# Grouping small matmuls of two side jobs: sums along heads in runs of five, transposes of a head pair in one run, and a wider spacing of a third group

## The chip, the cores and the metric

One core of one Trainium2 chip. The core has TensorE (PE, with its weight loads PEld), VectorE (DVE), ScalarE (ACT), GpSimd (POOL), SyncE (SP), which issues most DMAs, and 16 DMA engines. The metric is device time of one execution in microseconds; the median of three runs before the change is 1024.82 us (1024.57 to 1025.02).

## The reference

Two groups of tokens, 512 latent tokens and 128 context tokens (640 together), go through one layer of a hybrid backbone: a modulated norm, four gated mixers side by side (a short convolution, a bidirectional recurrence called HGRN2, attention, a chunked gMLP), an output projection and a ConvFFN. Everything is fp32. Only two mixers matter here.

```
cum    = cumsum(log_f)                                # per head, chunks of the sequence
scores = einsum('bhctd,bhcsd,bhctsd->bhcts', q, k, exp(cum_t - cum_s))
o      = scores @ v + (q * exp(cum)) @ state          # forward and, flipped, backward
o      = (o_f + flip(o_b)) * rsqrt(mean(o*o)) ; y_b = o * norm_g * silu(g)
```

```
s = concat(q @ k_window + bias, q @ k_context)        # 16 blocks: 4 heads x 4 column groups
p = softmax(s) ; y_c = p_window @ v_window + p_context @ v_context
```

## The kernel before, in words

Products are made exact enough by splitting each fp32 operand into a high part and a remainder, both stored as fp32r, and multiplying three times (high x high, high x remainder, remainder x high). The layer is a list of *units* that run one after another: the input projections (units 0 to 25: two column tiles for each of ff, fb, q, i, g, dv, du, ck, cq, cv, ac, ax, ab), some gates (26 to 29), one long unit of gate pairs in an order written out by hand (from 30), then the output projection and the FFN. A projection unit is `gemm` (L362): two halves of 320 columns, eight steps of three products each. Units i and dv are `tok_tile` (L933), with products of 256 columns and 20 steps each.

Between those products run *side jobs*, Python generators: `hgrn` (the recurrence), `gmlp`, `conva`, `attn`, `ada_cols` (modulation columns, one by one, as dot products on DVE at L262) and `g_operands`. What sets the order is a planner's clock `now`. A gemm step adds 0.41 to it (`tick(0.41)`), a step of `tok_tile` 0.33, and a side job's own PE work adds what `pe(...)` says. After each tick every job that is due is advanced to its next `yield`. A yield of `x` makes the job due `x` times its slack after the clock at which that step began (slack 1.3 for `hgrn`, 1.1 for `attn`, 1.0 for `ada_cols`):

```
def step(j):
    j[0] = now[0] + (next(j[1]) or 0.0) * j[2]
```

What is issued in this order is then placed on each engine by the framework's scheduler: it keeps the order where an instruction's operands are ready by its own model of time and pulls later instructions ahead where they are not. On the chip each engine then runs its list in order. `tc.keep_in_program_order` fixes some instructions; L262's are among them. From unit 30 to the end of the gate pairs everything is fixed.

The places that matter:

- `along` (L460 to L470) multiplies each of ten 128x128 blocks of a tensor by `heads`, a matrix of two columns. It sums a product of query and key along the 64 rows of each head. It runs twice: on `ksum` (tile D, during units 6 and 7) and on `near` (tile E, during units 8 and 9). Each of its ten matmuls is two passes on PE (it is fp32, not fp32r), each with its own weight load.
- Then come seven levels of the recurrence (L526, two or more groups of small matmuls each, and products on DVE at L545 and L549), the states (L565, L574), the outputs of five token tiles (L619 to L631), their norm (DVE L635 and L304, POOL L305, DVE L610), and the last transposes (L648): for each of five token tiles two transposes into the two halves of one PSUM tile, each followed by a product on DVE (L652).
- `ada_cols` stops after a column while `hgrn_y` is set and `hgrn_done` is not, that is from the last normed tile to the end of those transposes.
- `attn` waits for the end of `hgrn` and works in eight iterations, each for a pair of heads: `s3` of the pair before (L864 to L871), `s1` of the next pair (POOL L819, PE L827 and L830, DVE L834 and L836, ACT L837), and `s2` for each head of this pair: reciprocal and scaling on DVE (L843, L844), three transposes (L847) and a copy (DVE L1931 for one head, ACT L1929 for the other).

## Time and profile before

| | us |
|---|---|
| median of three runs | 1024.82 |
| the profiled execution's own time | 1023.97 |
| its span, first to last instruction | 1022.1 |
| PE busy | 1008.3 |
| DVE busy | 790.1 |
| first and last sum along heads (L466), start | 76.9 and 101.9 |
| first and last of the last transposes (L648), start | 198.7 and 203.6 (weight loads) |
| first and last of attention's transposes (L847), start | 228.2 and 283.0 (weight loads) |

The lists of the profile read: start in us, duration, engine, line, operation, output <- inputs, shape, count; in brackets the idle time before it and what ended it. A busy PE is not a PE at its peak: matmuls are pipelined, so what one costs is read from the starts of its neighbours. Lines are those of the kernel; a matmul issued in `gemm` is L362, in `tok_tile` L933.

### The profile page before, as it was taken

The numbers are of one execution on the slowest core, as the hardware profiler recorded it, in microseconds if no ns is written. First come the engines' busy times: TensorE is split into PE (matmuls) and PEld (weight loads), VectorE is DVE, ScalarE is ACT, GpSimd is POOL, SyncE is SP. The second block draws the span as 40 slices with busy tenths as digits, with TensorE's granted clock in tenths as the row PEclk, the third lists the DMA queues.
The fourth block names the chain that finished last, engine by engine and source line by source line (L and its number), as shares of the span: only waits on it lengthen the run. The fifth ranks groups of instructions, "written<-read, shape, count | busy, mean of one in ns | idle before, by whom it ended". The sixth has DMA issues, their size and how long they took to land.

```text
span 1022.1 us, 18764 instructions
## 1 busy us (share of the span) xinstructions
PE 1008.3 (99%) x7572; PEld 951.9 (93%) x7572; DVE 790.1 (77%) x1308; ACT 538.6 (53%) x933; POOL 106.5 (10%) x153
## 2 busy tenths in 40 slices
PE   8999999999999999999999999999999999999997
PEld 6899999999899999999998899999999999888886
DVE  6758899769866676767868879998888887796644
ACT  6642343354555444444544567777777776634432
POOL 1000020312100000000010111111112221001101
PEclk9999999999999999999999999999999999999999
DMA  9864433597562413323179584765555669974212
GB/s 354 322 221 127 126 124 114 171 263 216 143 206 79 155 52 104 130 77 104 49 282 349 207 328 112 195 163 150 150 151 149 154 161 271 370 259 146 83 42 103
DMA packets 55926, 177.85 MB, mean 174 GB/s; under 512 B 8192, under 2 KB 14624, under 8 KB 53280
## 3 DMA queue, kind: packets, MB, share of 16 engines
q1 hardware_dynamic: 45008, 140.60, 39.6%
q0 software_dynamic: 10832, 36.06, 14.8%
q8 instruction: 59, 0.97, 0.4%
q14 instruction: 27, 0.22, 0.1%
HBM read 134.93 MB, written 25.46 MB: 157 GB/s over the span
## 4 chain that ended last, share of the span: by engine, by line
PE 91%; DVE 5%; DMA 1%; issue 1%; ACT 1%; POOL 1%; SPq 0%; POOLq 0%; DVEq 0%; ACTq 0%
PE g L1478 19%; PE m L1122 17%; PE g L362 14%; PE g L1813 8%; PE m L1813 6%; PE g L1135 5%; PE m L1478 4%; PE m L1262 3%; PE g L933 2%; PE g L1262 2%; PE m L148 2%; PE g L148 1%; PE m L1473 1%; PE m L526 1%; DMA A<-in_w_ada_dram 1%
## 5 line engine op out<-in xcount | busy, mean ns | idle before, releaser
L362 PE MATMUL g<-XH,w 128*128 128x320 f32 x704 | 171.4, 317 | 0.0
L362 PEld LDWEIGHTS g<-XH,w 128*128 128x128 f32 x704 | 120.6, 188 | 2.4 <-issue 1.2
L362 PE MATMUL g<-XL,w 128*128 128x320 f32 x352 | 108.8, 309 | 0.0
L362 PEld LDWEIGHTS g<-XL,w 128*128 128x128 f32 x352 | 66.3, 188 | 0.0
L311 DVE TENSOR_TENSOR w<-raw,w 128x1024 fp32r<-128x1024 f32 x34 | 41.4, 1221 | 14.9 <-ACT w L310 9.1
L1122 PE MATMUL m<-XH,w 128*128 128x320 f32 x224 | 52.5, 309 | 0.0
L1813 PE MATMUL g<-w,XH 128*128 128x512 f32 (+1 forms) x216 | 50.2, 385 | 0.0
L1813 PEld LDWEIGHTS g<-w,XH 128*128 128x128 f32 x216 | 39.5, 188 | 8.3 <-ACT XH L1772 0.3
L310 ACT ACTIVATE w<-raw 128x1024 fp32r<-128x1024 f32 x34 | 35.7, 1050 | 21.3 <-PE g L1262 10.0
L1813 PE MATMUL g<-w,XL 128*128 128x512 f32 (+1 forms) x180 | 42.4, 386 | 0.0
L148 DVE SCALAR_TENSOR_TENSOR X<-MG,p2t,X 128x641 f32<-128x641 f32 x44 | 38.9, 885 | 4.3 <-ACT X L148 3.4
L148 DVE SCALAR_TENSOR_TENSOR X<-X,p2t,X 128x641 f32<-128x641 f32 x44 | 38.9, 884 | 1.9 <-ACT X L148 1.0
L1813 PEld LDWEIGHTS g<-w,XL 128*128 128x128 f32 x180 | 33.4, 188 | 7.1 <-DVE dt L1828 0.2
L148 ACT ACTIVATE w<-raw 128x1024 fp32r<-128x1024 f32 (+3 forms) x46 | 38.2, 851 | 2.7 <-DMA raw<-in_w_in_dram 1.7
L1478 PE MATMUL g<-XL,w 128*128 128x320 f32 x240 | 38.6, 310 | 0.0
L1478 PE MATMUL g<-XL,C 128*128 128x320 f32 x240 | 38.4, 309 | 0.0
L1122 PEld LDWEIGHTS m<-XH,w 128*128 128x128 f32 x224 | 38.3, 188 | 0.0
L1478 PEld LDWEIGHTS g<-XL,w 128*128 128x128 f32 x240 | 36.0, 188 | 0.5 <-ACT MG L148 0.3
L1813 PE MATMUL m<-w,XH 128*128 128x512 f32 (+1 forms) x156 | 36.4, 381 | 0.0
L1478 PEld LDWEIGHTS g<-XL,C 128*128 128x128 f32 x240 | 35.9, 188 | 0.4 <-ACT MG L148 0.4
L1122 PE MATMUL m<-XL,w 128*128 128x320 f32 x112 | 34.6, 309 | 0.0
L1813 PEld LDWEIGHTS m<-w,XH 128*128 128x128 f32 x156 | 28.5, 188 | 5.6
(549 smaller groups left out, 2751.9 us busy)
## 6 DMA issues: line engine op xcount, KB each, us to landing
raw<-in_w_up_dram SPq DMA_DIRECT2D x30, 512.0 KB, 4.9
raw<-in_w_gp_dram SPq DMA_DIRECT2D x21, 640.0 KB, 4.0
raw<-in_w_down_dram SPq DMA_DIRECT2D x22, 512.0 KB, 4.0
raw<-in_w_in_dram SPq DMA_DIRECT2D x19, 512.0 KB, 4.2
H<-in_w_adt_dram SPq DMA_DIRECT2D x16, 512.0 KB, 4.5
actd<-X POOLq DMA_DIRECT2D x22, 320.5 KB, 5.4
X<-in_w_adt_dram SPq DMA_DIRECT2D x10, 512.0 KB, 4.0
upd<-XL SPq DMA_DIRECT2D x4, 1280.0 KB, 6.4
```

The costliest lines, as they stand in the source:

```text
L148: r = f(*args, **kw)
L310: act(w[0], raw, AF.Copy)
L311: vec.tensor_tensor(w[1], raw, w[0].bitcast(F32), ALU.subtract)
L362: mm(o, w[:, h, k0 + k, :], r(k)[:, s], start=(k == 0 and i == 0), stop=(k == kt - 1 and i == 2))
L526: mm(m[W * g:W * g + W, (i - s0) * W:(i - s0 + 1) * W], lhs, rhs, start=True, stop=True, tile_position=(64 * par, W * g))
L933: mm(o, x(kx)[:, ts], w[:, h, k, :], start=(kx == 0 and i == 0), stop=(kx == 7 and i == 2))
L1122: mm(o, w[:, k, :], x[:, k, :], start=(first and k == 0 and j == 0), stop=(k == 3 and j == 2), skip_group_check=True)
L1135: mm(pb[:, c, 0:HC], w[:, h + k, :], y[:, x, k, s], start=(k == 0 and j == 0), stop=(k == 1 and j == 2))
L1262: mm(m, mh[k // 2][:, hx, k % 2, t * P:(t + 1) * P], wo[q][:, hw, k % 2, :], start=(k == 0 and i == 0), stop=(k == 7 and i == 2))
L1473: mm(o, w[:, k, :], x[:, k, :], start=(first and not part and k == 0 and j == 0), stop=(part == 1 and k == 3), skip_group_check=True)
L1478: z = mm(o, w[:, k, :], x[:, k, :], start=(first and k == 0 and j == 0), stop=(k == 3 and j == 2), skip_group_check=True)
L1813: mm(ps, sl[k][hx][:, t * P:(t + 1) * P], w[:, hw, k, c0:c1], start=first, stop=end and (last or nh == 1 and t == 4 and kk_ == 7))
```

## The change

Three places, no arithmetic changed:

- `along` issues its ten matmuls in two runs of five, with a yield of 2.5 after each run, where each had its own yield of 0.5.
- The last transposes of the recurrence yield 0.8 after each token tile instead of 0.4.
- In attention both heads' `s2` are issued in one step, 0.6 after the point where the first was issued before; the yields of an iteration still add up to 5.3 (1.5 + 0.6 + 3.2 for 1.5 + 1.2 + 1.2 + 1.4).

```diff
@@ along
             for i in range(10):
                 mm(mv[:, i, :], x[:, i * P:(i + 1) * P], heads, start=True, stop=True)
                 pe(0.22)
-                yield 0.5
+                if i % 5 == 4:
+                    yield 2.5
             return m
@@ hgrn, after the two transposes of a token tile
                 vec.scalar_tensor_tensor(s, m[:, pr * P:(pr + 1) * P],
                                          p1[:, C_HN + pr:C_HN + pr + 1], s, ALU.mult, ALU.mult)
-            yield 0.4
+            yield 0.8
         nc.sync.dma_start(ybd, split_y("D", sg).bitcast(F32))
@@ attn
             yield HD[6]
-            for i in range(2):
-                s2(u + i)
-                yield 1.2
-            yield HD[8] - 0.6
+            yield 0.6
+            s2(u)
+            s2(u + 1)
+            yield HD[8] + 1.2
         s3(14)
```

`HD[6]` is 1.5 and `HD[8]` is 2.0.

## The prediction

> **What bounds the kernel now.** I read the page's head first, then the list of PE's waits, then the order of time around the three places.

> ```profile
> span 1022.1 us, 18764 instructions
> PE 1008.3 (99%) x7572; PEld 951.9 (93%) x7572; DVE 790.1 (77%) x1308; ACT 538.6 (53%) x933; POOL 106.5 (10%) x153
> PE 91%; DVE 5%; DMA 1%; issue 1%; ACT 1%; POOL 1%; SPq 0%; POOLq 0%; DVEq 0%; ACTq 0%
> ```

> PE is busy 99% of the span and holds 91% of the chain that ended last. So the change can act in two ways only: through the PE time that its matmuls take among the fp32r products, and through stalls of PE. The span of 1022.1 belongs to an execution of 1023.97 us, 0.85 below the median of 1024.82; I add up against 1023.97 and put the 0.85 on at the end.

> The stalls at the lines concerned, first from the view of L648 (the recurrence's last transposes), then from that of L847 (attention's):

> ```profile
> L648 PEld LDWEIGHTS m<-cst,MG x10: 137/138/142, 198.6 to 203.6; 128*128 128x128 f32 x10
>   DVE MG L652: 2.3, 2
> ```

> ```profile
> L847 PEld LDWEIGHTS m<-cst,X x48: 137/139/143, 228.2 to 283.0; 128*128 128x128 f32 x48
>   DVE X L844: 1.4, 4
>   DVE X L834: 0.3, 1
> ```

> These rows count one wait twice, on PE and on its weight loads; the list of waits by engine separates them:

> ```profile
> PE m L648 <- DVE MG L652: 1.0, 1, 1.0
> PE m L847 <- DVE X L844: 0.4, 2, 0.2
> ```

> That leaves 1.3 us at L648 (2.3 - 1.0) and 1.3 at L847 (1.4 + 0.3 - 0.4), 2.6 us in all. The view of the sums (L466) lists no idle time. So 2.6 us, 0.25% of the time, is all that better places for these matmuls can win.

> **The sums in runs of five: the price of an interruption.** PE in order of time, columns start, duration, operation:

> ```profile
> 77.53 0.28 PE L933 MATMUL m<-w,XH 128*128 128x256 f32 x1
> 77.65 0.28 PE L466 MATMUL m<-heads,D 128*128 128x2 f32 x2
> 77.79 0.36 PE L933 MATMUL m<-w,XH 128*128 128x256 f32 x1
> 78.00 0.28 PE L933 MATMUL m<-w,XL 128*128 128x256 f32 x1
> 78.12 0.28 PE L933 MATMUL m<-w,XH 128*128 128x256 f32 x1
> ...
> 80.00 0.28 PE L933 MATMUL g<-w,XH 128*128 128x256 f32 x1
> 80.11 0.50 PE L466 MATMUL m<-heads,D 128*128 128x2 f32 x4
> 80.48 0.36 PE L933 MATMUL g<-w,XH 128*128 128x256 f32 x1
> 80.68 0.28 PE L933 MATMUL g<-w,XL 128*128 128x256 f32 x1
> ```

> Undisturbed products start 0.12 apart (78.00, 78.12). With one sum between them, two gaps take 78.00 - 77.53 = 0.47, so the sum costs 0.47 - 0.24 = 0.23. Here chance has put two sums side by side: 80.68 - 80.00 = 0.68, so the two cost 0.44, 0.22 each. A run saves 0.01 per sum at most. The loss after a run (0.20 to 0.21 to the second product instead of 0.12) is there, but inside the run each pass waits for its own weights as long (80.48 - 80.11 = 0.37 for four passes, 0.14 for two). If that goes on for five, twenty sums gain 20 x 0.01 = 0.2 us; from below I take 0, from above the 16 run ends that go, at 0.09 each: 1.4 us. I take 0.1, since two is the nearest row to five.

> The transposes follow the same law, one and four in a run:

> ```profile
> 198.56 0.31 PE L362 MATMUL g<-XH,w 128*128 128x320 f32 x1
> 198.71 0.27 PE L648 MATMUL m<-cst,MG 128*128 128x128 f32 x1
> 198.74 0.40 PE L362 MATMUL g<-XH,w 128*128 128x320 f32 x1
> 198.97 0.31 PE L362 MATMUL g<-XL,w 128*128 128x320 f32 x1
> 199.12 0.31 PE L362 MATMUL g<-XH,w 128*128 128x320 f32 x1
> 199.27 0.27 PE L648 MATMUL m<-cst,MG 128*128 128x128 f32 x1
> 200.56 0.33 PE L648 MATMUL m<-cst,MG 128*128 128x128 f32 x1 [1.02 <-DVE MG L652]
> ...
> 208.95 0.31 PE L362 MATMUL g<-XH,w 128*128 128x320 f32 x1
> 209.09 0.60 PE L749 MATMUL m<-cst,G 128*128 128x128 f32 x4
> 209.45 0.39 PE L362 MATMUL g<-XH,w 128*128 128x320 f32 x1
> 209.68 0.30 PE L362 MATMUL g<-XL,w 128*128 128x320 f32 x1
> ```

> Undisturbed gap 0.15 (198.97 to 199.12). One: 198.97 - 198.56 - 0.30 = 0.11. Four: 209.68 - 208.95 - 0.30 = 0.43, again 0.11 each. Eight runs of six instead of sixteen of three: 0 us, bound 8 x 0.08 = 0.6.

> **The sums also move the whole recurrence.** By the planner's arithmetic a sum in `tok_tile` was due 0.65 after its start; its own 0.22 and two ticks of 0.33 pass that, so ten sums took 20 ticks. Now a run of five is due 3.25 after its start; its own 1.10 leaves 2.15, seven ticks, 14 for both runs. In gemm steps (0.41) it was two ticks again (0.22 + 0.41 falls short of 0.65), 20 in all; now 2.15 takes six, 12 in all. With six and eight ticks gained and some rounding, everything behind the sums comes 10 to 16 ticks earlier; the last transposes start 15 ticks earlier. A gemm tick is three products of 0.15, so 198.7 becomes about 192. Nothing waits for `hgrn` there: the work of units 10 to 19 is PE's own, and `attn` starts after unit 19 as before. Cost: 0, as long as DVE keeps up; what moves is which DVE work meets which.

> **The last transposes, 0.8 apart.** In clock, one tile took its 0.22 and one tick; now two ticks. Why PE stopped there is in DVE's list:

> ```profile
> 195.56 0.42 DVE L610 TENSOR_TENSOR MG<-MG,hss 128x256 f32<-128x256 f32 x1 [0.99 <-POOL hss L305]
> 195.90 1.49 DVE L663 TENSOR_TENSOR E<-X,E 128x1280 fp32r<-128x1280 f32 x1
> 197.31 1.22 DVE L262 SCALAR_TENSOR_TENSOR junk<-H,S 128x1024 bf16<-128x1024 f32 x1
> 198.57 1.22 DVE L262 SCALAR_TENSOR_TENSOR H<-H,S 128x1024 f32<-128x1024 f32 x1
> ...
> 200.16 0.61 DVE L652 SCALAR_TENSOR_TENSOR MG<-m,cst,MG 128x128 f32<-128x128 f32 x2
> 200.93 0.35 DVE L652 SCALAR_TENSOR_TENSOR MG<-m,cst,MG 128x128 f32<-128x128 f32 x1 [0.17 <-PE m L648]
> ```

> The third transpose waits for the first product L652, because it is the second half of the first tile's PSUM tile, which DVE is reading. That product started 1.45 after its transpose (198.71 to 200.16), behind L663 and two column products L262. The wider spacing does not touch this first wait: both halves of a tile are still issued in one step, and the column job's products are still free to fill DVE. It even takes away the other tiles' transposes that stood between two halves. Free of a queue, transpose to transpose takes 200.93 - 200.56 + 0.35 = 0.72; if the scheduler leaves three products between (0.44 plus 0.08 for the switch), each later pair waits 0.2. So from 1.3 us the stall goes to between 0 (DVE free at once) and 1.3 + 4 x 0.2 = 2.1, or more if more columns lie ahead (rival below); I take 1.7, +0.4, since the DVE queue of the same make stands there.

> **Attention's pairs.** In the clock, an iteration loses one tick (three roundings instead of four), so the last of eight comes about seven ticks, 3 us, earlier; PE's own work is the same. The first head's scaling gets 0.66 more clock before its transposes, the second 0.66 less. Where PE waited, DVE was full:

> ```profile
> 249.00:272.00 23.00, 22.48 (x165) 19.67 (x165) 21.23 (x56) 10.24 (x22) 6.15 (x8) 1.00 0.63 168
> ```

> (PE, PEld, DVE, ACT, POOL busy, then PE's clock.) DVE is busy 21.23 of 23.00 us. By the clock the column products, issued in the same steps as each `s2` before and ahead of it, now come one to four ticks after it in the first half of the iterations, which helps; denser iterations on a full DVE hurt. Bounds: all 1.3 gone, or as much again; I take -0.3. Copies and PSUM buffers are the same in number.

> Sum: -0.1 (sums) + 0 (move) + 0.4 (last transposes) - 0.3 (attention) = 0.0. So 1023.97 + 0.0 + 0.85 = 1024.8.

> [...]

> ```profile
> 178.00:189.00 11.00, 11.00 (x96) 11.00 (x94) 8.69 (x28) 2.63 (x8) 2.02 (x2) 1.00 0.53 155
> 1016.00:1022.10 6.10, 0.00 (x0) 0.00 (x0) 1.45 (x5) 0.72 (x1) 0.55 (x1) 0.68 0.36 146
> ```

> The clock does fall in this trace, to a mean of 0.68 after PE's last product; it stays 1.00 in the stretch from 178 to 189, the recurrence's outputs, with 96 matmuls of many small kinds. [...]

> **Rivals.** *A, the waits go* (0.13). The recurrence leaves the crowded place, the two scalings come ahead of the column products, and all 2.6 us go: 1022.2. For it: the waits hang on one DVE queue each. Against: 21.23 of 23.00 us busy.

> *B, DVE is late for the last transposes* (0.11). In the clock the column job now stops before a column that it finished before the transposes, so two columns instead of one stand ready to fill DVE just before them. If both are placed there, the first L652 is two products of 1.22 later: +2.4, and four later pairs at 0.2 bring 0.8: 3.2 more, 1028.0. It decides once the first L652 starts over 3 us after its transpose (1.45 now). Against: the scheduler fills only what it holds idle.

> *C, runs are cheap after all* (0.04): the 0.08 to 0.09 at each run's end goes, 16 x 0.09 + 8 x 0.08 = 2.0: 1022.8, or 0.2%. Against: the rows for two sums and four transposes.

> *D, PE's clock halves in the runs* (0.02): four runs of sums (1.1 each) and eight of transposes (0.67 each) take twice as long: 9.8, so 1034.6. Against: clock 1.00 in 178 to 189.

> **How the numbers follow.** The forecast, no change beyond 0.2% (about what a measurement of this kernel can tell from no change, 2.05 us), has 0.70: its terms are bounded by waits of 1 to 2 us each. Faster by over 0.2% is A, 0.13. Slower is B and D, 0.13. Within is the rest, 0.74, C at the edge included. The range of 1022.6 to 1027.4 takes in the bounds of the terms (2.6 down less a little, 0.8 + 1.3 up with some of B) and leaves out the far ends of A and B, and D.

> **What would show it.** Runs of ten passes at L466, 0.11 apart, with 0.22 for each sum: the price. L648 starting near 192 instead of 198.7: the move. A wait of PE for L652 of 1 to 2 us: the queue; none is A, over 3 is B. Six-fold rows at L847 with waits for L844 of together about 1 us. A stall of over 1 us at L526 or anywhere else between 70 and 290 that is not there now, or a start of the gate pairs moved by over 2 us, makes the prediction wrong.

## The result and the profile after

The changed kernel takes 1031.26 us (median of five executions, 1028.05 to 1032.82) against 1024.65 us before, measured beside it: the ratio is 1.0060 (95% interval 1.0048 to 1.0071). The prediction was 1024.8, with a range of 1022.6 to 1027.4. The profiled execution is the longest of the five; its span grew from 1022.1 to 1031.0 us, 8.9 us.

The head of its page, and from its list of PE's waits (total, times, longest) the two rows that matter here. The lines of the changed kernel below L468 have moved down by one: L527 is L526 of before, L649 is L648, L848 is L847.

```profile
span 1031.0 us, 18769 instructions
PE 1015.4 (98%) x7572; PEld 957.6 (93%) x7572; DVE 789.0 (77%) x1308; ACT 538.7 (52%) x933; POOL 110.8 (11%) x153
```

```profile
PE m L649 <- DVE MG L653: 2.3, 2, 1.4
PE m L527 <- DVE C L546: 1.6, 2, 1.1
```

There are the same 7572 matmuls, but PE's busy time grew by 7.1 us (1008.3 to 1015.4): the matmuls took longer. A wait at L527, the recurrence's levels, is new; that at L649 grew from 1.0 to 2.3 us; L848, attention's transposes, is no longer in the list.

Where the time went shows in busy time by stretch. The columns are the length, then PE, PEld, DVE, ACT and POOL with their instructions, PE's granted clock (1.00 is full speed), the DMA share and GB/s. The changed kernel first:

```profile
104.00:146.70 42.70, 42.60 (x1040) 39.98 (x1039) 37.20 (x67) 19.27 (x38) 7.22 (x6) 1.00 0.37 115
146.70:150.20 3.50, 1.95 (x27) 1.48 (x26) 3.50 (x6) 0.17 (x1) 0.00 (x0) 0.99 0.49 150
150.20:160.40 10.20, 10.20 (x86) 8.97 (x87) 5.92 (x12) 3.32 (x9) 0.00 (x0) 0.50 0.33 104
```

and the same stretches of the kernel before:

```profile
146.70:150.20 3.50, 3.50 (x27) 3.31 (x27) 3.50 (x6) 1.83 (x5) 0.00 (x0) 1.00 0.58 193
150.20:160.40 10.20, 10.20 (x148) 8.37 (x145) 9.24 (x21) 5.07 (x12) 0.00 (x0) 1.00 0.49 157
```

From 104 to 146.7 PE is as busy as before (42.60 us in both) and gets through as many matmuls (1041 before). Then PE stands for 1.6 of 3.5 us, and for the next 10.2 us its clock is granted at 0.50: 86 matmuls instead of 148, of several sizes. PE is busy all through these 10.24 us, so I put the price of half speed at half of them, 5.1 us. That is an estimate, and a little high for the products of `gemm`: three of them take 0.80 us there (156.40 to 157.20) where they take 0.44 at 1.00 (146.13 to 146.57), which by 0.36 of 0.80 gives 4.6.

The sum goes by two milestones, two of ACT's copies out of PSUM, here of the kernel before and then of the changed one:

```profile
103.67 0.71 ACT L409 ACTIVATE MG<-g 128x640 f32<-128x640 f32 x1 [0.68 <-PE g L362]
217.46 0.70 ACT L418 ACTIVATE MG<-g 128x640 f32<-128x640 f32 x1 [0.41 <-PE g L362]
```

```profile
104.19 0.71 ACT L409 ACTIVATE MG<-g 128x640 f32<-128x640 f32 x1 [0.90 <-PE g L362]
226.96 0.71 ACT L418 ACTIVATE MG<-g 128x640 f32<-128x640 f32 x1 [0.40 <-PE g L362]
```

By 104 us, when all sums along heads are done, it is 0.5 late; at the start of attention 9.5; at the end 8.9. So the 9.0 us are lost in between: 1.6 of waits at L527, 5.1 of clock, 2.3 - 1.0 = 1.3 of waits at L649. About 1 us is left (1.5 with 4.6 for the clock) that I cannot put on one place. After that 0.6 comes back: the last sigmoid of the gates stands at 317.85 against 309.49, 8.4 late, so the stretch with attention gives back 1.1, and 0.5 is lost again behind it.

The other four executions differ mostly in the clock. Their times and mean granted clocks are 1028.05 (0.998), 1029.05 (0.999), 1031.26 (0.995) and 1031.53 (0.995), and the profiled one 1032.82 (0.993). A mean clock that is lower by 0.003 is 3.1 us of 1031, one lower by 0.005 is 5.2. So by this estimate two executions kept their clock, two lost about 3 us to it and one 5; only the last has a trace. With the clock kept, the change costs 3.4 to 4.4 us; the rest is what the clock does.

**Why PE stopped at L527.** PE in order of time in the changed kernel, and below it DVE:

```profile
147.01 0.31 PE L362 MATMUL g<-XH,w 128*128 128x320 f32 x1
148.46 0.32 PE L527 MATMUL m<-C,B 64*64 64x64 f32 x2 [1.14 <-DVE C L546]
149.20 0.79 PE L527 MATMUL m<-C,B 64*64 64x64 f32 x18 [0.41 <-DVE C L546]
```

```profile
138.36 0.31 DVE L550 TENSOR_TENSOR A<-A 128x80 f32<-128x80 f32 x1
141.16 1.23 DVE L324 TENSOR_TENSOR w<-raw,w 128x1024 fp32r<-128x1024 f32 x1 [2.49 <-ACT w L323]
142.30 1.31 DVE L262 SCALAR_TENSOR_TENSOR junk<-H,S 128x1024 bf16<-128x1024 f32 x1
...
146.03 1.64 DVE L546 TENSOR_TENSOR B<-B,A 128x640 f32<-128x640 f32 x2
147.59 1.55 DVE L546 TENSOR_TENSOR C<-C,A 128x640 f32<-128x640 f32 x2
```

The last level (the 64x64 matmuls) needs four products of DVE, L546, which end at 149.14 (147.59 + 1.55). They stand behind three column products L262, and these behind L324, a weight's remainder, for which DVE sat idle 2.49 us: it needs ACT's copy L323. On ACT, changed kernel and then before:

```profile
137.05 2.99 ACT L542 ACTIVATE MG<-D 32x640 f32<-32x640 f32 x4 [1.68 <-DVE D L532]
140.06 1.06 ACT L323 ACTIVATE w<-raw 128x1024 fp32r<-128x1024 f32 x1
```

```profile
132.50 1.05 ACT L323 ACTIVATE w<-raw 128x1024 fp32r<-128x1024 f32 x1
139.14 2.99 ACT L541 ACTIVATE MG<-D 32x640 f32<-32x640 f32 x4 [3.31 <-DVE D L531]
```

The recurrence has moved forward past a weight's conversion: L323 used to stand ahead of the four copies of L542 and now stands behind them. So DVE delivers the block at about the same time as before (147.80 + 1.55 = 149.35 there), although the recurrence as a whole lies earlier. But PE has nothing left ahead of the level from 147.3 on, where it came to it at 152.4 before:

```profile
147.80 1.55 DVE L545 TENSOR_TENSOR C<-C,A 128x640 f32<-128x640 f32 x2
152.39 0.80 PE L526 MATMUL m<-C,B 64*64 64x64 f32 x20
```

**Why PE stopped longer at L649.** DVE around the last transposes of the changed kernel:

```profile
201.24 0.35 DVE L653 SCALAR_TENSOR_TENSOR MG<-m,cst,MG 128x128 f32<-128x128 f32 x1
203.30 1.23 DVE L262 SCALAR_TENSOR_TENSOR junk<-H,S 128x1024 bf16<-128x1024 f32 x1 [1.71 <-DMA H<-in_w_adt_dram]
204.45 0.60 DVE L653 SCALAR_TENSOR_TENSOR MG<-m,cst,MG 128x128 f32<-128x128 f32 x2
```

The first wait is that of before. The second is new: a column product got into DVE's queue between the first and the second product L653, and the weights that it reads had not landed. DVE stood 1.71 us for a DMA with the second and the third L653 behind it, and PE, at its fifth transpose (205.11), stood 1.43 us for the third.

### The profile page after: what moved, and what is told of

Read it like the earlier page. It is cut to its first block, busy times and chain, and to the rows that moved or that the text cites. A ratio compares the mean times of both kernels' runs of the same rounds, so it can differ in the third digit from the quotient of the medians.

```text
span 1031.0 us, 18769 instructions
## 1 busy us (share of the span) xinstructions
PE 1015.4 (98%) x7572; PEld 957.6 (93%) x7572; DVE 789.0 (77%) x1308; ACT 538.7 (52%) x933; POOL 110.8 (11%) x153
## 4 chain that ended last, share of the span: by engine, by line
PE 78%; issue 9%; DVE 5%; DMA 4%; ACT 2%; POOL 1%; SPq 1%; POOLq 0%; DVEq 0%; ACTq 0%
PE g L1479 19%; PE m L1123 17%; PE g L362 9%; PE g L1814 8%; PE m L1814 5%; PE g L1136 5%; PE m L1479 4%; PE m L1263 3%; PE g L1263 2%; PE m L1474 1%; DMA B<-in_w_ada_dram 1%; DMA S<-in_w_ada_dram 1%; DMA C<-in_w_ada_dram 1%; DVE D L586 1%; DVE junk L262 1%
## 5 line engine op out<-in xcount | busy, mean ns | idle before, releaser
L362 PE MATMUL g<-XH,w 128*128 128x320 f32 x704 | 171.8, 320 | 0.1
L362 PEld LDWEIGHTS g<-XH,w 128*128 128x128 f32 x704 | 122.1, 191 | 2.9 <-issue 1.0
L362 PE MATMUL g<-XL,w 128*128 128x320 f32 x352 | 110.4, 314 | 0.0
L362 PEld LDWEIGHTS g<-XL,w 128*128 128x128 f32 x352 | 67.3, 191 | 0.1
L323 ACT ACTIVATE w<-raw 128x1024 fp32r<-128x1024 f32 (+1 forms) x22 | 24.3, 1104 | 18.9 <-issue 8.8
```

The lines of the kernel that those rows point to most:

```text
L323: high = lambda: act(w[:, 0], raw, AF.Copy)
L362: mm(o, w[:, h, k0 + k, :], r(k)[:, s], start=(k == 0 and i == 0), stop=(k == kt - 1 and i == 2))
```

## The experiments

Each was timed in five rounds beside the kernel before, whose median was 1024.24 to 1024.39 us in all four series. Ratios are to the kernel before, with their 95% intervals.

**The sums in runs alone** (first part of the diff).

```diff
-                yield 0.5
+                if i % 5 == 4:
+                    yield 2.5
```

> The sums' part of the change alone: two runs of five with a yield of 2.5 after each, the transposes as before. Theory 'place': the loss is in where the recurrence comes to lie (14 to 16 planner steps earlier), so most of the 6.6 us stay: 1028 to 1032, with a stop of PE at L526 before its last level and executions in which PE's clock falls for about 10 us. Theory 'later parts': the loss is the spacing's and attention's, and this kernel stays within 1 us of 1024.7. Theory 'runs': as 'place' in time, told apart by e2 and e3.

1039.61 us, 1.0153 (1.0129 to 1.0177): this part alone costs 15.3 us, more than twice the whole change and well over the 1028 to 1032 that I expected. Its waits:

```profile
PE g L362 <- ACT gt L972: 3.4, 1, 3.4
PE m L865 <- DVE B L1932: 2.8, 1, 2.8
PE m L649 <- DVE MG L653: 2.5, 2, 1.6
PE m L527 <- DVE C L546: 1.3, 2, 0.8
```

The lower two are those of the changed kernel; the upper two are not in it. PE's clock falls behind two of the stops, for 6.83 and 3.41 us. ACT's order around the first wait:

```profile
292.07 0.28 ACT L871 ACTIVATE C<-m 128x128 fp32r<-128x128 f32 x1 [1.51 <-PE m L865]
296.35 0.42 ACT L148 ACTIVATE H<-raw 128x256 fp32r<-128x256 f32 x1 [4.00 <-DMA raw<-in_w_gp_dram]
296.78 1.28 ACT L972 ACT_TABLE_LOAD   x1
298.07 0.79 ACT L972 ACTIVATE gt<-g,cst 128x640 f32<-128x640 f32 x1
```

The gate's sigmoid, which must free a PSUM tile for PE, stands behind a copy whose DMA is late by 4.00 us.

**The same runs, in place**: longer yields, so that the recurrence stays where it was.

```diff
-        def along(x):
+        def along(x, wait):            # 3.3 for ksum, 3.9 for near
-                yield 0.5
+                if i % 5 == 4:
+                    yield wait
```

> Runs of five, but with yields of 3.3 and 3.9 after each, so that the planner reaches everything behind the sums at the same step as before (along ends at its 85th and 119th step in both). Theory 'place': 1024.4 to 1025.0, the price of a sum unchanged at 0.22 us and no new stop. Theory 'runs' (five sums in a row cost PE time or PE's clock): as slow as e1, 1028 to 1032.

1024.74 us, 1.0002 (0.9993 to 1.0011). There is no wait at the levels or the gate, attention's transposes wait 1.0 us (0.4 before), and the clock stays at 1.00 from its first rise to the last product. A run of five costs and saves nothing that this measurement can tell.

**Single sums, moved**: no runs, but yields short enough for the recurrence to come forward as in the first experiment.

```diff
-                yield 0.5
+                yield 0.5 if i % 5 in wait else 0.2      # wait: (1, 3) for ksum, (2,) for near
```

> Each sum alone among the fp32r products, but with shorter yields, so that the recurrence lies exactly where the runs put it (along ends at steps 79 and 106, as in e1). Theory 'place': 1028 to 1032 as e1, with the same stop before the last level. Theory 'runs': 1024 to 1025.5.

1034.75 us, 1.0095 (1.0079 to 1.0112), again over the 1028 to 1032 that I expected. DVE's idle time before L324 is there (2.46 us), and so is the stop at the gate:

```profile
PE g L362 <- ACT gt L971: 3.1, 1, 3.1
PE m L648 <- DVE MG L652: 1.8, 1, 1.8
```

With the run in place there is no loss, without runs but moved there is one: it is the move. Only the stop at L526 did not come. DVE's rows and the start of the level on PE show why not:

```profile
139.68 1.23 DVE L324 TENSOR_TENSOR w<-raw,w 128x1024 fp32r<-128x1024 f32 x1 [2.46 <-ACT w L323]
145.16 1.55 DVE L545 TENSOR_TENSOR C<-C,A 128x640 f32<-128x640 f32 x2
147.03 0.80 PE L526 MATMUL m<-C,B 64*64 64x64 f32 x20
```

L324 starts 1.5 us earlier than in the changed kernel, and two column products stand between it and the block instead of three. So the block is done at 146.71, and PE comes to the level at 147.03. DVE's idle time behind ACT is therefore not enough for the stop: it takes that and what DVE has queued in front of the block.

**Attention's pair alone** (third part).

> Attention's part alone: both heads' transposes in one step. From the trace of the changed kernel, whose delay shrinks by 0.6 us over attention and which lists no wait at attention's transposes any more: 0.3 to 1.3 us faster, 1023.4 to 1024.4. The forecast had put -0.3 on it; a rival with a fuller DVE: up to 1.3 us slower.

1024.97 us, 1.0004 (0.9995 to 1.0012): not the gain that I expected. The waits at L847 stay at 0.3 us in the list (0.4 before), and one of 1.1 us for the copy of DVE appears at the next place, `PE m L864 <- DVE B L1931`.

**The spacing alone** (second part).

> The kernel before with the last transposes 0.8 apart and nothing else changed. Theory (the loss comes from where the sums leave the recurrence, the spacing only moves four pairs by 0.2 us each): the waits at the last transposes stay within 0.5 us of before's 1.3 us, no fall of the clock, 1024.0 to 1025.5 us. Rival (the spacing moves the planner's later work onto a late buffer or DMA by itself): over 1026 us, with a new wait of over 1 us behind the last transposes.

1025.83 us, 1.0012 (1.0003 to 1.0021), in its profile 1.7 us of waits at L847 where there were 0.4, and no other new wait near the change. It is 0.3 over what I expected.

**The changed kernel, last level later.** `l` counts the levels from 0 to 6; the step behind level 5 waits 2 us more.

```diff
-            yield HD[1]
+            yield HD[1] + (2 if l == 5 else 0)
```

> The changed kernel with the recurrence's last level due 2.0 us later, so that DVE's block for it is done when PE comes to it. Theory (the stop of PE before the last level costs 1.9 us and the 10.2 us at half clock behind it 5.1 us): the waits of L527 on L546 (1.6, 2, 1.1) go, the clock stays at 1.00 between 150 and 190 us, and of the 6.6 us lost at least 4 come back: 1025.5 to 1027.5 us. Rival (the clock falls for another reason, such as the runs of five): the row of 150 to 190 us keeps a clock near 0.87 and the time stays over 1029 us.

1026.92 us (1025.93 to 1030.44), 1.0028 (1.0018 to 1.0039): of 6.6 us lost 4 come back. PE now comes to the level at 150.5, the wait at L527 is gone, and the clock behind it stays up:

```profile
146.70:150.20 3.50, 3.50 (x26) 3.50 (x25) 3.50 (x6) 0.00 (x0) 0.00 (x0) 1.00 0.48 150
150.20:160.40 10.20, 10.20 (x144) 7.79 (x143) 8.03 (x16) 5.21 (x12) 0.00 (x0) 1.00 0.31 106
196.30:199.70 3.40, 1.15 (x9) 0.88 (x8) 3.33 (x7) 0.00 (x0) 2.40 (x3) 1.00 0.93 208
199.70:203.10 3.40, 3.40 (x16) 3.29 (x15) 2.25 (x8) 0.00 (x0) 1.22 (x1) 0.50 0.96 280
```

The profiled execution (1030.44, the longest of its seven) shows the same thing at another place: a stop of 2.25 us at the last transposes and 3.41 us at half clock right behind it. The first product L653 starts there 2.7 us after its transpose (196.00 to 198.70), behind three column products: that comes close to the prediction's rival B, which put its mark at 3 us, though in another kernel. The six other executions lie at 1025.9 to 1027.4, against 1028.05 and 1029.05 of the changed kernel where that kept its clock, so about 2 of the 4 us are the stop and the rest is the clock that no longer falls.

**The kernel before, last level earlier**, by 2.5 us and then by 4.5.

```diff
-            yield HD[1]
+            yield HD[1] - (2.5 if l == 5 else 0)      # 4.5 in the second
```

> The kernel before with the recurrence's last level due 2.5 us earlier and the sums as they were. Theory (a level that PE reaches before DVE has its block is enough to stop PE, and the stop takes the clock with it): a wait of L526 on L545 of 1 to 2 us, then 3.4 to 10.2 us at half clock, 1027 to 1031 us. Rival (the stop costs itself alone): the wait is there, the clock stays at 1.00, 1025 to 1026.5 us.

> The kernel before with the recurrence's last level due 4.5 us earlier. Moved by 2.5 it started 3.3 us earlier, at 149.07, just when DVE's block was done (149.4). Theory (PE ahead of DVE's block stops, and a stop of over 1.2 us in one stretch of 3.41 us among the level's small matmuls halves the clock for some multiple of 3.41 us): waits of L526 on L545 of together 1 to 2 us before 150 us, a clock of 0.5 behind them in the profiled or in some other execution, and executions that lie in two groups about 3 us apart. Rival (the stop in the changed kernel came from the sums in runs themselves): no wait at L526.

1031.23 us, 1.0067 (1.0054 to 1.0080), and 1035.86, 1.0111 (1.0098 to 1.0125). The first time lies 0.2 above the range I gave, and for another reason; both expectations failed in their point. There is no wait at L526 in either. The level starts at 149.07 in the first and 148.78 in the second, 2 us more of yield having moved it by 0.3. I read this as the framework's scheduler holding it until its own model has DVE's block ready, with a model that is right where the 2.49 us behind ACT are missing; no run tests that. What the two runs show is that an earlier yield alone does not make the stop. The rival of the second expectation, that the sums in runs make it, foresaw just this, and every trace with the stop has the sums in runs. Against it stand the runs left in place and the level 2 us later, both with runs of five and without the stop. The loss of these two kernels lies further on, at the gate in both and in attention in the second:

```profile
PE m L864 <- DVE B L1931: 4.1, 1, 4.1
PE g L362 <- ACT gt L971: 3.0, 1, 3.0
```

**The changed kernel without one of its other parts**: the spacing back to 0.4, or attention's transposes one by one.

> The changed kernel with the last transposes 0.4 apart again: the sums in runs and the attention's pair, without the spacing. If the spacing is what takes part of the sums' loss back: the stop at L362 on ACT gt L972 of about 3 us comes back and the time is over 1033 us. If the attention's pair does it: 1029 to 1032 us as the changed kernel, without such a stop, and the waits of L649 on L653 change by under 1 us.

> The changed kernel with attention's transposes one by one again: the sums in runs and the spacing, without the pair. If the pair is what takes part of the sums' loss back: waits behind 250 us return (L865 on B of 2 to 3 us, or the stop at L362 on ACT gt L972 of about 3 us), and the time is 1034 to 1040 us. If the spacing does it: 1029 to 1032 us with no such wait.

1031.95 us, 1.0065 (1.0053 to 1.0077), and 1030.95, 1.0066 (1.0053 to 1.0079): the same as with all three. The executions of both lie in two groups, 1029.0 to 1029.6 with mean clocks of 0.998 and 0.999, and 1032.0 to 1033.2 with 0.993 to 0.996. Either of the two parts takes back some 8 us of the 15.3 that the sums cost alone, and no gate stop is left in either. ACT's order in the second shows how:

```profile
285.65 0.28 ACT L871 ACTIVATE C<-m 128x128 fp32r<-128x128 f32 x1 [2.21 <-PE m L865]
285.95 1.28 ACT L972 ACT_TABLE_LOAD   x1
287.24 0.80 ACT L972 ACTIVATE gt<-g,cst 128x640 f32<-128x640 f32 x1
...
295.30 0.40 ACT L148 ACTIVATE H<-raw 128x256 fp32r<-128x256 f32 x1
```

The sigmoid stands ahead of the copy. The two go together in all sixteen traces: the copy stands first in four (the sums alone, the single sums moved, the level earlier by 2.5 and by 4.5), each with a stop at the gate of 3.0 to 3.7 us; the sigmoid stands first in the other twelve, and none has that stop. That the order makes the stop I read from the rows; no run turns that order round by itself.

**Both last transposes of a tile ahead of their two products**, in the kernel before, then in the changed kernel.

```diff
             for pr in range(2):
                 ten.transpose(m[:, pr * P:(pr + 1) * P], ...)
                 pe(0.11)
+            for pr in range(2):
                 s = sg[...]
                 vec.scalar_tensor_tensor(s, m[:, pr * P:(pr + 1) * P], ...)
```

> The kernel before with both transposes of a tile issued ahead of the two products of L652, so that the second one does not wait for DVE to read the first. Theory (the waits of L648 on L652 are PE standing behind DVE and cost what they last): these waits fall from 1.3 us to under 0.3 us and the time with them, 1023.0 to 1023.9 us. Rival (what PE gains there it gives back at the next wait for DVE, in attention): 1024.3 to 1024.8 us, with a wait at L847 or L864 that has grown by about 1 us.

> The changed kernel with both of the last transposes of a tile ahead of the two products of L653. Theory (of the 6.6 us lost some 1 to 1.5 us are PE standing behind DVE's queue at the last transposes, and the stop at L527 with its clock is untouched): the waits of L649 on L653 fall from 5.7 to about 1 us, the stop at L527 and a clock of 0.5 behind it stay, 1028 to 1030.5 us. Rival (PE waits there for a DVE that is late anyway, so that what is gained goes into the next wait): 1030.5 to 1032 us.

In the kernel before 1023.23 us, 0.9987 (0.9978 to 0.9995): the wait of 1.0 us at L648 is gone, and 1.0 us of time with it; the interval ends below 1, so a gain of about 0.1% is shown. In the changed kernel 1027.22 us (1026.26 to 1031.13), 1.0039 (1.0024 to 1.0053), better than the 1028 I gave as the lower end: the waits of PE at L649 fall from 2.3 to 1.0 us (with those of its weight loads the changed kernel has 5.2, not the 5.7 of the expectation). Its profile has stops of 0.6 and 0.4 us at L527 and no fall of the clock. Part of the gain is that clock: four of the six executions keep it (1026.3 to 1027.6), where two of five did in the changed kernel (1028.05 and 1029.05). So the edit itself is worth some 1.5 to 2 us there.

**That edit and attention's pair, in the kernel before.**

> The kernel before with both last transposes of a tile ahead of their products, and attention's transposes of a pair in one run (part 3 of the change), the sums as they were. If the two waits for DVE are separate: 1.0 us less than before from the first and up to 0.4 us from the second, 1022.6 to 1023.4 us. If the pair's transposes only move a wait (as alone, where L864 on B took 1.1 us): 1023.2 to 1024.3 us.

1023.42 us, 0.9990 (0.9981 to 0.9998), with 1.4 us of waits for B at L865: the pair moves a wait and adds nothing.

**The changed kernel with both stops taken out**: the last level 2 us later and both transposes first.

> The changed kernel with the last level due 2.0 us later and both last transposes of a tile ahead of their products, all three parts of the change in place. Theory (the two stops and the clock behind them are all that the change lost): both waits are gone or under 0.5 us, no fall of the clock, 1023.5 to 1025.5 us. Rival (something else of the move costs as well): 1026 us and more, with a wait elsewhere.

1024.34 us (1023.35 to 1025.76), 1.0001 (0.9992 to 1.0010). Nothing is waited for at L527 or L649, and the clock holds:

```profile
146.70:160.40 13.70, 13.70 (x168) 11.25 (x167) 11.52 (x21) 5.21 (x12) 0.00 (x0) 1.00 0.35 116
```

All three parts of the change are in this kernel, so the two stops, with the clock behind them, are nearly all of the loss. Not quite all: the edit of the transposes also took 1.0 us off the kernel before, and against that kernel (1023.23) the change still costs about 1 us, which is open. The profile has a wait of 1.6 us in the FFN (L1815 on a product of DVE) that the other lacks; whether that is it no run shows.

## Why the prediction was wrong

*What bounds the kernel: right, but short.* It said that the change can act in two ways only, PE's time and PE's stalls. A third was missing: PE's clock as a result of a stall. By the estimate above it took 5.1 of the 8.9 us in the profiled execution. The 2.6 us of stalls were read from the weight loads' waits (1.3 and 1.3); PE's own were 1.0 and 0.4, and taking the first one away brought 1.0.

*The price of a run: right.* In the changed kernel the five sums of one run stand between 80.44 and 81.80:

```profile
80.44 0.28 PE L934 MATMUL g<-w,XH 128*128 128x256 f32 x1
80.56 1.18 PE L466 MATMUL m<-heads,D 128*128 128x2 f32 x10
81.59 0.36 PE L934 MATMUL g<-w,XH 128*128 128x256 f32 x1
81.80 0.28 PE L934 MATMUL g<-w,XL 128*128 128x256 f32 x1
```

81.80 - 80.44 = 1.36; less two gaps of 0.12 that is 1.12 for five sums, 0.22 each as before, and the run left in place made no difference. The longer run made no pass cheaper.

*The move: here it failed.* Its size was right, as the groups of levels 5 and 6 show, before and after:

```profile
L526 PE MATMUL m<-C,B x240: 192/196/267, 143.9 to 157.3; 64*32 64x32 f32 x80, 64*64 64x64 f32 x40
```

```profile
L527 PE MATMUL m<-C,B x240: 192/196/366, 139.5 to 154.9; 64*32 64x32 f32 x80, 64*64 64x64 f32 x40
```

They began 4.4 us earlier, 10 gemm ticks of 0.44, where 10 to 16 were predicted. The last transposes came 15 ticks earlier, just as predicted: 537 products of `gemm` lie ahead of the first one, 582 before. They start at 199.9 and not near 192 because the kernel had lost nearly 8 us by then. Its price was not right: "Cost: 0, as long as DVE keeps up; what moves is which DVE work meets which." I named the condition and did not test it against DVE's and ACT's lists. The recurrence's own copies on ACT were moved past a weight's conversion, DVE waited for that with three column products queued behind it, and the level waited for DVE. It was worth 1.6 us of waits in the profiled execution and 5.1 of clock; of the other four, two lost about 3 us of clock, behind which stop no trace shows. The prediction's last part named a stall at L526 as what would prove it wrong, and that is the one that came; it had no price in the sum and no chance among the rivals.

*The last transposes: first wait right, second missed.* The prediction took the stall from 1.3 to 1.7 us, with a bound of 2.1. Counted as there, at the weight loads, it went from 1.3 to 2.8; PE's own wait grew from 1.0 to 2.3. The first wait stayed, as said. The second is near rival B, a column product in front of L653, but it was late for a DMA and not for DVE's own time. And the spacing did not bring it: alone it left the wait at 1.0 us, and without it the changed kernel still has 2.1.

*Attention: nothing.* -0.3 was taken; alone the pair made no difference that can be told. In the changed kernel the stretch with attention gave 1.1 us back, but the pair alone did not, so that is not shown to be the pair's.

*Rival D had the clock, for a wrong reason.* It let runs of sums and transposes halve it. No trace has a fall of the clock at such a run: every fall inside the work comes after a step of 3.41 us (see the end) in which PE was idle for 1.25 us or more.

## What to carry to other kernels

Where a planner's clock sets the order, an edit of a few yields moves a whole job past other work on every engine: compare the order on ACT and DVE, not only PE, and ask which instruction now stands behind one that waits. With PE at 99%, price a stop at what it lasts plus the clock that it may take along: here the stops that were followed by a fall left PE idle for 1.25 to 2.80 us of a step of 3.41 us, and the fall lasted 3.41 to 10.24 us, of which I count half. Idle time of 1.78 and 1.83 us in a step had no fall behind it, so a trace has to show it. See also whether executions of the same kernel lie in groups 3 us apart. Issuing the transpose into the second half of a tile ahead of the product that reads the first half took 1.0 us off here.

## What the runs showed of the hardware that I had not expected

| stretch (us) | kernel | PE idle | clock behind it |
|---|---|---|---|
| 146.74 to 150.16 | changed, last level | 1.55 | 0.5 for 10.24 |
| 147.11 to 150.53 | sums alone, last level | 1.25 | 0.5 for 6.83 |
| 145.91 to 149.33 | without spacing, last level | 0.98 | 1.0 |
| 256.34 to 259.75 | sums alone | 2.80 | 0.5 for 3.41 |
| 289.65 to 293.07 | single sums moved | 2.76 | 0.5 for 3.41 |
| 196.32 to 199.73 | level later | 2.25 | 0.5 for 3.41 |
| 194.08 to 197.49 | single sums moved | 1.82 | 0.5 for 3.41 |
| 194.45 to 197.86 | level 2.5 earlier | 1.83 | 1.0 |
| 293.89 to 297.30 | sums alone | 1.78 | 1.0 |
| 199.02 to 202.44 | before | 1.02 | 1.0 |

The three falls that are not in the table followed 2.18 and 2.40 us of idle time (the level 4.5 earlier, each 6.83 us at 0.5) and 2.76 (the level 2.5 earlier, 3.41 us). Among the projections' products a step with 1.82 us of idle time had a fall behind it, steps with 1.78 and 1.83 had none; around the last level 1.25 and 1.55 had one, 0.98 had none. That the small matmuls there make the difference is my reading, from three steps. What sets whether a fall lasts one, two or three steps stays open. A stop of 3.4 us in the sums alone, at 295, was cut by a border into 1.78 and 1.62 and cost no clock. The first rise lay between 4.5 and 7.6 us after the span's first instruction from one trace to the next, so by my reading the same stop can fall whole into one step in one execution and be cut in two in the next. That fits the groups of times; only the profiled executions have a trace, so for the others it is a reading of their times and mean clocks.

In none of the steps before a fall inside the work was PE idle throughout: 2.80 of 3.41 us was the most and 1.25 the least.
